# An encoder trunk on one core: the first projections of the sample before its norm, in an order written out by hand, and layer norm's last step on ScalarE

## The chip, the core and the metric

One core of one Trainium2 chip runs one launch of the whole network. The core has TensorE (PE, with its weight loads PEld), VectorE (DVE), ScalarE (ACT), GpSimd (POOL) and SyncE (SP, which here only issues transfers). The metric is the device time of the launch in microseconds. Everything is fp32 in memory; a product of two fp32 matrices is made on PE as three products of "high" and "low" parts (`hi` x `hi`, `lo` x `hi`, `hi` x `lo`), where `hi` is the number rounded to the fp32r format by an ACT copy, and `lo` what is left of it, by a subtraction on DVE or POOL.

## The reference, cut to what matters

There are two groups of tokens, a prompt of 1024 and a sample of 256, which pass the same layer. What the change touches is the layer's beginning:

```python
def rmsnorm(x, w):
    return x * lax.rsqrt(jnp.mean(x * x, -1, keepdims=True) + EPS) * w

h = rmsnorm(x, norm_mix_w)
proj = h @ w_in                     # columns: qkv, ab, dn_gate, sg_u, sg_v, gate_a, gate_b
...
u = gelu(sg_u)
v = layernorm(gelu(sg_v), ln_w, ln_b)
mixed = einsum('gts,bnsgc->bntgc', w_s, v) + b_s    # per chunk of 128 tokens
return u * mixed
```

The rest (gated DeltaNet over the qkv columns, branch gates, cross-attention into 256 memory tokens, a SwiGLU layer and a last norm) is the same in both kernels.

## The kernel before

**Tiles.** The model's 1024 features lie in `KT` = 8 slices `k` of 128 partitions, tokens along the free dimension. Tokens come in three blocks: `x0` and `x1` (512 tokens of the prompt each, blocks 0 and 1) and `xs` (the sample, block 2). `x_h[b]` holds the normed block as `hi` and `lo`. Chunks `c` are 128 tokens: 0 to 3 in block 0, 4 to 7 in block 1, 8 and 9 in block 2.

**The first stage.** It makes the sg_v columns and the 16 `ab` columns, with tokens as output rows (`sgv`, weights `w_sv` in two halves of 264 columns, tiles `svh`/`svl`), then the sg_u columns with features as output rows (`sgu(g, b)`, four weight tiles `w_u`). A chunk and half of `sgv` is a chain of 24 products of 264 columns into one PSUM bank (8 slices x 3), a tile and block of `sgu` one of 24 products of 512 or 256 columns. `gelu2` takes a bank out: a square on ACT, a step on DVE, a tanh on ACT, a step on DVE, which leaves `vg` (or `ug`). `ln` is the layer norm of `vg`: sums, four squares with accumulation on ACT, a root by Newton steps on DVE (`rsqrt`, ten tiny instructions), and at L458 the scaling of each chunk on DVE. `mix` multiplies a group of `vg` by the mixing weights `sw` on PE and ends in a store to `ybd`.

**A block's norm.** Squares on ACT are added up on DVE (`nacc`), PE sums them over partitions (a product with the column of ones, `bank<-cst,nacc`), DVE makes the root (`nst`), PE broadcasts it over the partitions (`bank<-cst,nst`), DVE scales each slice (`nt`, L285), ACT rounds it to `hi` and DVE or POOL subtracts for `lo` (`split`, L125 and L126; odd slices on DVE, even ones on POOL). `first_norm` does this for the sample at once; `other_norms` does block 0, then block 1, then the memory, beside the products.

**What sets the order.** PE's order is what the program writes. Main generators (`sgv`, `sgu`) yield after each slice, and side generators (norms, layer norms, mixes) are taken up when a clock that adds up nominal PE time has passed their due time (`K.clock`, `pump`; numbers such as `yield 3000` and `LAG0` are nanoseconds of it). `K.until` moves this clock on until a side generator has come to a point. The order on DVE, ACT, POOL and SP is made by a scheduler, from the program's order and estimated times. Each engine takes its instructions in order. The stage goes: `sgv` of the sample, `bias`, `sgu(0, 2)`, `sgu(1, 2)`; `sgv(0)`, `sgu(0, 0)`, `sgu(1, 0)`; `sgv(1)`, `decays`, `sgu(0, 1)`, `sgu(1, 1)`; then the tiles 2 and 3 for all blocks.

**Buffers.** PSUM banks for these products come from two pools of four (`pm` for `sgv` and `sgu`, `pq` for the rest). Raw weights have two buffers, `whi`/`wlo` two each, `nsq`/`nt` three, an x block one.

## Time and profile before

| | |
|---|---|
| time, median of 3 runs | 2236.44 us (2235.29 to 2237.58) |
| the profiled execution | 2239.41 us |
| its span | 2237.6 us |
| mean granted clock of PE | 0.996 |
| PE waits in the first 240 us, by releaser: DVE `nacc`, DMA `cst`, ACT `hi`, POOL `svl` | 8.6, 2.4, 2.3, 2.0 us |
| DMA over the span | 117 GB/s |

The profile is one execution: every instruction with its start and length, and for a wait the event that ended it. A group names the line in the code, the engine, output and inputs by their names in the program, and the shape. A line can be a helper's: L108 is every product, L125 and L126 every split. "Busy" of PE is a modelled figure in which neighbouring products overlap, so the step from one start to the next says more than a length. The granted clock says which share of TensorE's full clock the chip gave.

### The profile page before, as it was taken

To read this page: it belongs to the slowest core of one execution; us is meant where nothing else is said; L and a number is where in the kernel's file an instruction comes from. 1 tells how busy PE (TensorE), PEld (TensorE's weight loads), DVE (VectorE), ACT (ScalarE), POOL (GpSimd) and SP (SyncE) were. 2 spreads that over 40 slices of the span, in tenths; PEclk is the share of its full clock that TensorE was granted. 3 is DMA by queue.
4 is the path that set the end of the run, shared out by engine and by line. 5 is a ranking of instruction groups with operands and counts; after the bars stand their busy time and mean duration, and the time that the engine had idled before them with its cause. 6 is when DMAs were issued, how large, how long until landed. Compare 5 with 4: busy or idle time off the path is not lost.

```text
span 2237.6 us, 32329 instructions
## 1 busy us (share of the span) xinstructions
PE 2186.0 (98%) x12416; PEld 1909.1 (85%) x12416; DVE 1439.1 (64%) x2796; ACT 829.3 (37%) x1481; POOL 559.9 (25%) x358
## 2 busy tenths in 40 slices
PE   6999999999999999999999999999999999999998
PEld 5988888888888899788888888888888888888888
DVE  7767788897985874588844536743444344478575
ACT  5434143333423443124544433432223223243453
POOL 3010000000000000025331332466666666200031
PEclk9999999999999999999999999999999999999999
DMA  5222322214234454981431342222222222393531
GB/s 180 82 80 74 104 72 83 73 62 112 68 103 128 149 150 129 314 283 47 152 103 48 137 162 78 67 104 85 83 86 80 76 83 90 134 355 127 202 109 57
DMA packets 192821, 263.52 MB, mean 118 GB/s; under 512 B 72394, under 2 KB 102682, under 8 KB 192666
## 3 DMA queue, kind: packets, MB, share of 16 engines
q1 hardware_dynamic: 172826, 232.34, 31.7%
q10 hardware_dynamic: 19840, 29.11, 3.6%
q8 instruction: 97, 1.59, 0.3%
q14 instruction: 58, 0.48, 0.1%
HBM read 183.24 MB, written 78.16 MB: 117 GB/s over the span
## 4 chain that ended last, share of the span: by engine, by line
PE 77%; DVE 10%; issue 5%; DMA 4%; ACT 2%; POOL 1%; SPq 0%; ACTq 0%; POOLq 0%; DVEq 0%
PE bank L108 76%; DMA tbd<-stage 1%; PE bank L121 1%; DVE acc L615 1%; DVE xf L126 1%; DVE W L761 1%; DVE wlo L126 1%; DMA braw<-gq 1%; DVE x L1437 1%; DVE wlo L1228 1%; DMA t<-sgd 0%; DVE sw L919 0%; DVE W L764 0%; DVE U L861 0%; DVE lo L126 0%
## 5 line engine op out<-in xcount | busy, mean ns | idle before, releaser
L108 PE MATMUL bank<-hi,whi 128*128 128x512 f32 (+1 forms) x1976 | 701.8, 355 | 0.0
L108 PE MATMUL bank<-hi,wlo 128*128 128x512 f32 (+1 forms) x1976 | 687.0, 348 | 0.0
L108 PE MATMUL bank<-lo,whi 128*128 128x512 f32 (+1 forms) x1976 | 686.8, 348 | 0.0
L108 PEld LDWEIGHTS bank<-hi,wlo 128*128 128x128 f32 x1976 | 373.5, 189 | 48.8
L108 PEld LDWEIGHTS bank<-hi,whi 128*128 128x128 f32 x1976 | 374.4, 189 | 43.9 <-issue 0.2
L108 PEld LDWEIGHTS bank<-lo,whi 128*128 128x128 f32 x1976 | 374.5, 190 | 43.3 <-issue 0.2
L125 ACT ACTIVATE whi<-raw 128x1024 fp32r<-128x1024 f32 (+1 forms) x136 | 137.1, 1010 | 262.8 <-PE bank L108 221.4
L126 POOL TENSOR_TENSOR wlo<-raw,whi 128x1024 fp32r<-128x1024 f32 x65 | 157.5, 2426 | 302.8 <-ACT whi L125 302.8
L108 PE MATMUL bank<-bhl,whi 128*128 128x512 f32 x408 | 125.9, 390 | 0.0
L126 DVE TENSOR_TENSOR wlo<-raw,whi 128x1024 fp32r<-128x1024 f32 (+1 forms) x71 | 81.6, 1151 | 43.7 <-ACT whi L125 36.7
L126 POOL TENSOR_TENSOR wlo<-x,whi 128x1024 fp32r<-128x1024 f32 x40 | 97.5, 2436 | 46.8 <-ACT whi L125 46.7
L2009 DVE TENSOR_TENSOR x<-x,bank 128x512 f32<-128x512 f32 x21 | 14.4, 688 | 125.3 <-ACT x L1804 125.3
L108 PEld LDWEIGHTS bank<-bhl,whi 128*128 128x128 f32 x408 | 76.4, 188 | 16.3 <-ACT whi L125 0.3
L615 DVE SCALAR_TENSOR_TENSOR acc<-craw,sm,acc 128x510 f32<-128x510 f32 (+1 forms) x96 | 73.5, 766 | 20.5 <-ACT acc L613 19.1
L1817 DVE SCALAR_TENSOR_TENSOR t<-t,x 128x512 f32<-128x512 f32 x42 | 64.4, 1534 | 28.4 <-ACT t L1816 28.4
L108 PE MATMUL bank<-bhl,wlo 128*128 128x512 f32 x204 | 79.6, 390 | 0.5 <-DVE wlo L126 0.5
L761 DVE TENSOR_TENSOR W<-W,UT 128x2 f32<-128x2 f32 (+30 forms) x155 | 73.0, 471 | 11.0 <-DMA W<-in_eye 6.7
L250 DVE TENSOR_TENSOR nacc<-nacc,nsq 128x512 f32<-128x512 f32 (+1 forms) x68 | 57.9, 852 | 34.5 <-ACT nsq L249 33.4
L125 ACT ACTIVATE whi<-x 128x1024 fp32r<-128x1024 f32 (+1 forms) x48 | 49.0, 1025 | 79.9 <-PE bank L108 73.7
L1826 DVE SCALAR_TENSOR_TENSOR t<-bank,t 128x512 f32<-128x512 f32 (+1 forms) x44 | 24.5, 558 | 82.6 <-PE bank L108 82.6
L978 ACT ACTIVATE gs<-bank 128x512 f32<-128x512 f32 (+1 forms) x60 | 31.2, 520 | 124.9 <-PE bank L108 119.6
L881 POOL COPY UT<-U 64x512 f32<-64x512 f32 x20 | 13.9, 699 | 247.2 <-PE bank L108 245.6
(372 smaller groups left out, 4606.6 us busy)
## 6 DMA issues: line engine op xcount, KB each, us to landing
raw<-in_w_gu SPq DMA_DIRECT2D x44, 512.0 KB, 3.4
braw<-gq SPq DMA_DIRECT2D x14, 1024.0 KB, 6.5
raw<-in_w_g SPq DMA_DIRECT2D x20, 512.0 KB, 3.3
gq<-t SPq DMA_DIRECT2D x33, 256.0 KB, 2.0
gtd<-gs ACTq DMA_DIRECT2D x32, 256.0 KB, 2.0
w<-in_w_dn SPq DMA_DIRECT2D x8, 1024.0 KB, 12.3
raw<-in_w_qkv SPq DMA_DIRECT2D x12, 512.0 KB, 3.5
gq<-r SPq DMA_DIRECT2D x22, 256.0 KB, 2.1
```

What stands on the lines that cost most here:

```text
L108: self.nc.tensor.matmul(out, l, r, start=start, stop=stop, skip_group_check=more)
L121: self.nc.tensor.transpose(out, x, ident)
L125: self.last_hi = self.nc.scalar.activation(hi, src, AF.Copy).ins
L126: (eng or self.nc.vector).tensor_tensor(out=lo, in0=src, in1=f32(hi), op=ALU.subtract)
L250: (eng or V).tensor_tensor(out=self.acc, in0=self.acc, in1=sq, op=ALU.add)
L615: V.scalar_tensor_tensor(out=dst, in0=src, scalar=wj, in1=dst, op0=ALU.mult, op1=ALU.add)
L761: V.tensor_tensor(out=t3, in0=u3[:, i:, c:].rearrange("p j c -> p c j"), in1=XL[:, 32 * i + i : 32 * i + 32].unsqueeze(1).to_broadcast([P, ...
L978: S.activation(t, ps, AF.Tanh, scale=0.5)
L1228: eng.tensor_tensor(out=hl[1], in0=self.raw[*src, x], in1=f32(hl[0]), op=ALU.subtract)
L1437: V.scalar_tensor_tensor(out=d, in0=ps, scalar=0.5, in1=d, op0=ALU.mult, op1=ALU.add)
L1817: V.scalar_tensor_tensor(out=t, in0=t, scalar=1.0, in1=src, op0=ALU.add, op1=ALU.mult)
L1826: V.scalar_tensor_tensor(out=out, in0=u, scalar=sign, in1=t, op0=ALU.mult, op1=ALU.mult)
```

## The change

The sample's first projections are made from x * w, not from the normed h: rounding x times the norm's weight needs no root. The root of the token's mean square is multiplied in when the bank is read (`sample_evac`: a copy within PSUM scaled per partition; `gate_evac2`: a product with the broadcast root `rb2`). All of the stage from the first load up to the first half of `sgv(0)` stands in one stretch, `begin`, in which the orders on ACT, DVE, POOL and SP are also as the program writes them. In it the first half's raw weights are loaded from ACT's queue, the products of a group of banks run with slice `k` outermost (`sv_mm` over two chunks of the sample, over all four of block 0), and `sgu(0, 2)` and `sgu(1, 2)` come before block 0's products. The sample's own `hi` and `lo` of h are made later, by `other_norms`, ahead of x1's norm; block 0's norm is written out in the stretch. `LAG0` goes, and block 1 gets a lag `LAG1`. In `ln` the scaling becomes an ACT instruction, `Identity` with scale and bias, after one more tiny DVE step.

```diff
-            V.tensor_scalar(out=vg[:, c, :], in0=vg[:, c, :], scalar1=mu[:, c : c + 1], scalar2=rs[:, c : c + 1], op0=ALU.subtract, op1=ALU.mult)
+        V.scalar_tensor_tensor(out=mu[:, cs], in0=mu[:, cs], scalar=-1.0, in1=rs[:, cs], op0=ALU.mult, op1=ALU.mult)
+            S.activation(vg[:, c, :], vg[:, c, :], AF.Identity, scale=rs[:, c : c + 1], bias=mu[:, c : c + 1])
...
+    def sv_mm(pss, x, cols, w, k):
+        wh, wl = wk(w, k, 264)
+        for ps, cs in zip(pss, cols):
+            for n, (l, r) in enumerate(((x[0][:, k, cs], wh), (x[1][:, k, cs], wh), (x[0][:, k, cs], wl))):
+                mm(ps[:, :264], l, r, k == 0 and n == 0, k == KT - 1 and n == 2)
...
+    begin.enter_context(tc.manual_schedule(engines={S.engine, V.engine, G.engine, SY.engine}))
...
+    SY.dma_start(sm, a["small"])
+    for i, raw in enumerate(sv_raw0):
+        S.dma_start(raw, a["w_sv"][0][:, i * 1056 : (i + 1) * 1056])
...
+    for k in range(KT):
+        S.activation(xw[:, 0, k, :], xs[:, k, :], AF.Copy, scale=w_mix(k))
+        V.scalar_tensor_tensor(out=xw[:, 1, k, :], in0=xs[:, k, :], scalar=w_mix(k), in1=f32(xw[:, 0, k, :]), op0=ALU.mult, op1=ALU.subtract)
+    hl = sv_tiles()
+    for i in range(2):
+        sv_split(i, sv_raw0[i], hl)
...
+    ps2 = [[bank(pm) for _ in range(2)] for _ in range(2)]
+    for k in range(6):
+        sv_mm(ps2[0], x2w, cols2, sv[0], k)
...
+    u2(0)
+    pc0, nb0 = rstd_bank([sq0.acc], 512)
+    u2(1)
...
+    def sample_evac(half, i, ps):
+        c, nv = chunks(2)[i][0], 264 if half == 0 else 248
+        S.activation(ps[:, :264], ps[:, :264], AF.Copy, scale=y2[:, i : i + 1])
+        yield from gelu_of(ps[:, :nv], vg[:, c, half * 264 : half * 264 + nv], nv, (s0 if half == 0 else s1)[:, c : c + 1])
+        if half:
+            V.tensor_copy(ab[:, c, :], ps[:, 248:264])
...
+    go(0, 1, 0, 1)
+    rstd_col(pc0, nb0, y0)
+    go(2, 0, 1)
+    pb0 = rstd_rows(y0, 4)
+    steps = [(2,), (3,), (2,), (3, 4), (4, 3), (5, 4), (5,), (5,)]
...
+    for k in range(KT):
+        t = xp.tile([P, 512], F32, tag="nsq", name="nt", bufs=3)
+        V.scalar_tensor_tensor(out=t, in0=x0[:, k, :], scalar=w_mix(k), in1=pb0, op0=ALU.mult, op1=ALU.mult)
...
+        go(*steps[k])
...
+    V.tensor_scalar(out=h05, in0=sm[:, S_DNW : S_DNW + 9], scalar1=0.5, scalar2=None, op0=ALU.mult)
+    V.tensor_scalar(out=bias2, in0=bias2, scalar1=0.5, scalar2=None, op0=ALU.mult)
+    ps0 = [bank(pm) for _ in range(4)]
+    for k in range(KT):
+        sv_mm(ps0, x_h[0], [cs for _, cs in chunks(0)], sv[0], k)
+    begin.close()
...
+    def other_norms():
+        x1_ = x_load(a["xT"], 512, 512, "x1")
+        for k in range(KT):
+            t = xp.tile([P, 512], F32, tag="nsq", name="nt", bufs=3)[:, :NS]
+            V.scalar_tensor_tensor(out=t, in0=xs[:, k, :], scalar=w_mix(k), in1=rb2, op0=ALU.mult, op1=ALU.mult)
+            to_h(x_h, 2)(k, t)
+            yield 1500
+        done.add(2)
+        yield from norm(xp, lambda k: x1_[:, k, :], 512, S_MIX, to_h(x_h, 1), 900, lag=LAG1)
...
+    bias()
+    K.main(sgv(0, (1,)))
+    for b in (0, 1):
+        if b:
+            K.main(sgv(1))
+            K.side(decays())
+        K.main(sgu(0, b))
+        K.main(sgu(1, b))
...
-LAG0, LAGF, LAGF2, PACEF = 7500, (8000, 6000, 1500), (9000, 9000, 2800), 1000
+LAG1, LAGF, LAGF2, PACEF = 4000, (8000, 6000, 1500), (9000, 9000, 2800), 1000
```

How instructions move, at three places (a row is line, operation, output and inputs with buffer numbers, shape, and how often it repeats).

PE at the start, before: the mean square of the sample (`nacc`) and the broadcast of its root (`nst`), then one chunk's products with the normed `hi2` and `lo2`.

```order
L108 MATMUL bank_135<-cst_74,nacc_124 128x1 x4
L108 MATMUL bank_152<-cst_74,nst_140 128x128 x2
L108 MATMUL bank_212<-svh_104,hi2_101 128x264
L108 MATMUL bank_212<-svh_104,lo2_102 128x264
L108 MATMUL bank_212<-svl_103,hi2_101 128x264
```

PE at the start, now: `xw` is x * w, both of its parts under one name.

```order
L108 MATMUL bank_180<-svhi_162,xw_108 128x264 x2
L108 MATMUL bank_180<-svlo_163,xw_108 128x264
L108 MATMUL bank_181<-svhi_162,xw_108 128x264 x2
L108 MATMUL bank_181<-svlo_163,xw_108 128x264
L108 MATMUL bank_180<-svhi_162,xw_108 128x264 x2
L108 MATMUL bank_180<-svlo_163,xw_108 128x264
```

The two statistics groups moved behind products, and two banks take turns slice by slice.

DVE at the scaling of block 0 (`nt`, from `x0` and the broadcast in a bank), now: between the pieces stand the sample's gelu (`gt`, `vg`, `ug`) and the copies of `ab` out of the banks of its second half, `bank_182` and `bank_183`.

```order
L694 SCALAR_TENSOR_TENSOR nt_436<-x0_116,sm_75,bank_419 128x512
L700 TENSOR_TENSOR lo0_111<-nt_430,hi0_110 128x512
L663 SCALAR_TENSOR_TENSOR vg_100,sums_101<-gt_415,bank_182 128x248
L670 COPY ab_99<-bank_182 128x16
L694 SCALAR_TENSOR_TENSOR nt_443<-x0_116,sm_75,bank_419 128x512
L660 SCALAR_TENSOR_TENSOR gt_434<-gt_434,bank_183 128x248
L677 TENSOR_TENSOR ug_448<-bank_338,rb_119 128x256
L694 SCALAR_TENSOR_TENSOR nt_452<-x0_116,sm_75,bank_419 128x512
L700 TENSOR_TENSOR lo0_111<-nt_443,hi0_110 128x512
L660 SCALAR_TENSOR_TENSOR gt_450<-gt_450,ug_448 128x256
L663 SCALAR_TENSOR_TENSOR vg_100,sums_101<-gt_434,bank_183 128x248
L670 COPY ab_99<-bank_183 128x16
```

Before, only the sample's gate gelu and its layer norm stood between the pieces, and all of the sample's `sgv` banks were out by then.

PE at the mean square of x1, before: it stands (`nacc_556`) amid the products of block 0's second half, `bank_676`.

```order
L108 MATMUL bank_676<-svh_119,hi0_97 128x264
L108 MATMUL bank_676<-svh_119,lo0_98 128x264
L108 MATMUL bank_676<-svl_118,hi0_97 128x264
L108 MATMUL bank_692<-cst_74,nacc_556 128x1 x4
L108 MATMUL bank_676<-svh_119,hi0_97 128x264
L108 MATMUL bank_676<-svh_119,lo0_98 128x264
```

PE at the mean square of x1, now: it is `nacc_825`, the broadcast of its root is `nst_929`, and `hi1` and `lo1` are what this norm makes.

```order
L108 MATMUL bank_878<-hi0_110,whi_332 128x512
L108 MATMUL bank_878<-lo0_111,whi_332 128x512
L108 MATMUL bank_878<-hi0_110,wlo_333 128x512
L108 MATMUL bank_924<-cst_74,nacc_825 128x1 x4
L108 MATMUL bank_941<-sw_103,vg_100 128x128 x4
L108 MATMUL bank_950<-cst_74,nst_929 128x128 x4
L108 MATMUL bank_959<-sw_103,vg_100 128x128 x4
L108 MATMUL bank_1001<-svhi_162,hi1_112 128x264
L108 MATMUL bank_1001<-svhi_162,lo1_113 128x264
L108 MATMUL bank_1001<-svlo_163,hi1_112 128x264
```

It moved behind the last product of `sgu(1, 0)` (`bank_878`); between it and the first product with `hi1` stand only two mixes and the broadcast.

More of the change, by code (lines that the diff above doesn't have):

```diff
@@ L537, in bias @@
     def bias():
-        V.tensor_scalar(out=bias2, in0=bias2, scalar1=0.5, scalar2=None, op0=ALU.mult)
         pw = bank()
@@ L566, in sgu @@
         yield from proj(ps, ws[g], x_h, b)
[L567 removed]
+        if (g, b) in ((0, 1), (2, 2), (3, 2)):
             K.ahead()
@@ new lines, in rstd_rows, with __init__, square, add @@
+    def rstd_rows(y, nb):
+        pb = bank()
+        for c in range(nb):
+            mm(pb[:, c * P : (c + 1) * P], y[:, c : c + 1].to_broadcast([P, P]), ident)
+        return pb
+    class Squares:
+        def __init__(self):
+            self.acc = xp.tile([P, 512], F32, tag="nacc", name="nacc", bufs=2)
+            self.rest = []
+        def square(self, x):
+            t = self.acc if not self.rest else xp.tile([P, 512], F32, tag="nsq", name="nsq", bufs=3)
+            S.activation(t, x, AF.Square)
+            self.rest.append(t)
+        def add(self, k):
+            V.tensor_tensor(out=self.acc, in0=self.acc, in1=self.rest[k], op=ALU.add)
@@ new lines, in trunk_kernel @@
+    for k in range(4):
+        sv_mm(ps2[1], x2w, cols2, sv[1], k)
+    pb2 = rstd_rows(y2, 2)
+    for k in range(4, KT):
+        sv_mm(ps2[1], x2w, cols2, sv[1], k)
+    K.split_w(0)
+    for k in range(4, KT):
+        sq0.square(x0[:, k, :])
+        sq0.add(k - 2)
+    S.activation(rb2, pb2[:, :NS], AF.Copy)
+    K.lo_vector = True
+    sq0.add(6)
+    sq0.add(7)
+    K.split_w(1)
+    K.lo_vector = False
+    for g in range(2):
+        ws.append(K.take())
+    pu2 = [bank()[:, :NS] for _ in range(2)]
@@ L582, in trunk_kernel @@
         K.main(sgu(1, b))
+    K.until(norms, lambda: 2 in done)
     for g in (2, 3):
```

215 lines of the change are left out of this document (134 added, 81 removed).

## The prediction

> **What bounds the kernel now.** I read the page's engine line first, then the table of windows over the first 133 us (columns: stretch, length, busy us of PE, PEld, DVE, ACT and POOL with their instructions, granted PE clock, DMA share, GB/s), then the PE rows there in order of time, and last the groups by form.
>
> ```profile
> span 2237.6 us, 32329 instructions
> PE 2186.0 (98%) x12416; PEld 1909.1 (85%) x12416; DVE 1439.1 (64%) x2796; ACT 829.3 (37%) x1481; POOL 559.9 (25%) x358
> ...
> 0.00:16.00 16.00, 3.27 (x13) 2.92 (x13) 7.30 (x19) 6.65 (x9) 2.81 (x6) 1.00 0.86 301
> 16.00:44.40 28.40, 24.77 (x162) 22.99 (x163) 23.74 (x57) 17.07 (x35) 13.48 (x9) 0.94 0.37 129
> 44.40:57.00 12.60, 10.07 (x53) 8.58 (x52) 10.61 (x29) 6.89 (x15) 2.93 (x2) 0.73 0.46 158
> 57.00:115.60 58.60, 58.25 (x439) 55.91 (x439) 46.00 (x134) 27.75 (x61) 5.53 (x4) 1.00 0.24 88
> 115.60:133.00 17.40, 16.00 (x83) 13.03 (x82) 15.30 (x52) 8.28 (x18) 4.96 (x2) 1.00 0.17 58
> ```
>
> PE is busy for 98% of the span, so only what PE loses can be won, and most of it is lost in the first 57 us: in the three windows there PE is busy 38.1 of 57.0 us, partly at a lowered clock (0.94, 0.73). From 57 us on it is full. The change rewrites just this beginning. The order of the built programs differs on PE up to its instruction 620, the first product of `sgu(0, 1)`; from there PE's rows are the same in both. So I ask one thing: when does PE reach that instruction, which I call S? These rows of PE's timeline tell it for the kernel before (columns: start, duration, instruction, idle time before it and its releaser):
>
> ```profile
> 15.79 0.59 PE L108 MATMUL bank<-svh,hi 128*128 128x264 f32 x1 [1.79 <-ACT hi L125]
> ...
> 27.76 0.39 PE L108 MATMUL bank<-svl,hi 128*128 128x264 f32 x1 [2.03 <-POOL svl L126]
> ...
> 30.05 0.42 PE L108 MATMUL bank<-svl,hi 128*128 128x264 f32 x1
> 30.27 0.42 PE L108 MATMUL bank<-svh,hi 128*128 128x264 f32 x1
> ...
> 51.63 0.59 PE L108 MATMUL bank<-svh,lo 128*128 128x264 f32 x1
> ...
> 55.74 0.28 PE L108 MATMUL bank<-svh,lo 128*128 128x264 f32 x1
> 55.86 0.29 PE L108 MATMUL bank<-svl,hi 128*128 128x264 f32 x1
> ...
> 65.24 0.95 PE L108 MATMUL bank<-cst,nacc 128*128 128x1 f32 x8
> ...
> 87.09 0.39 PE L108 MATMUL bank<-hi,whi 128*128 128x512 f32 x1
> 87.32 0.39 PE L108 MATMUL bank<-lo,whi 128*128 128x512 f32 x1
> ...
> 115.62 0.40 PE L108 MATMUL bank<-hi,whi 128*128 128x512 f32 x1
> ```
>
> The reader sees four things. The first projection starts at 15.79, after the mean square and its root. S is at 115.62. A 264-column product follows the one before it by 0.12 us (55.74, 55.86), and by 0.22 us where the clock is low (30.05, 30.27); a 512-column one by 0.227. And after a stall the low clock stays on: dense work resumes at 51.63 and has the short step only from 55.74, 4.1 us later; half of that, some 2 us of work, is lost.
>
> **The start.** The first projection now takes x*w and needs no root: it needs the small table, all four pieces of the sample's x and the first half of the weights, whose two loads move to ACT's queue.
>
> ```profile
> GB/s 0 0 81 291 328 232 327 249 268 293 349 352 369 394 401 406 412 401 388 391 347 414 382 363 227 108 176 281 205 46 0 0 0 0 0 0 0 0 131 360
> ...
> raw<-in_w_sv SPq DMA_DIRECT2D x4, 528.0 KB, 6.4
> ...
> xs<-in_xT SPq DMA_DIRECT2D x4, 256.0 KB, 3.7
> ...
> sm<-in_small SPq DMA_DIRECT2D x1, 54.5 KB, 4.2
> ```
>
> That is 4 x 256 + 2 x 528 + 54.5 KB, 2.19 MB. The GB/s row has 0.75 us slots; its running sum reaches 2.08 MB at 9.0 us and 2.19 at 9.3. At the later rate of some 400 it would be 7.0. Then come two last ACT pieces of x*w, the weight's high half on ACT and its low half on DVE; the groups of ACT by form (busy, mean ns of one) and a row of DVE's timeline give their prices:
>
> ```profile
> L125 ACT ACTIVATE hi<-nt 128x512 fp32r<-128x512 f32 x16 | 9.9, 631 | 6.9 <-DVE nt L285 6.7
> ...
> L125 ACT ACTIVATE svh<-raw 128x1056 fp32r<-128x1056 f32 x4 | 4.3, 1075 | 3.1 <-DMA raw<-in_w_sv 3.1
> ...
> L125 ACT ACTIVATE hi<-nt 128x256 fp32r<-128x256 f32 x8 | 3.2, 413 | 4.5 <-DVE nt L285 4.5
> ```
>
> ```profile
> 28.18 1.25 DVE L126 TENSOR_TENSOR svl<-raw,svh 128x1056 fp32r<-128x1056 f32 x1
> ```
>
> With x in at 9.0, a little ahead of the weights on the other queue, the first product stands at 10.7 (two pieces 0.7, the high half 1.08) and dense work begins a low half later: 12.0; by 400 GB/s it is 10.1. I take 11.8, since the slots up to 9 us are the nearest rows and some of the split lies under the last load. In the page "DMA: Bandwidth & Descriptors", section "Issuing engines are not separate DMA queues", the Trainium skill says that loads issued by several engines run on the same 16 DMA engines and interleave, and only the issuing time is saved; by that the move to ACT's queue brings nothing to 11.8, and no run here yet shows two such queues at the start.
>
> Up to the end of the broadcast of block 0's root PE then has 142 products (17.1), two mean groups and two broadcasts (2.6, an estimate from 0.95 us for the group of four at 65.24, half for the sample's), and about 22 products at the low clock (22 x 0.1 = 2.2): 33.7. Squares, splits and the new readout by the root (four ACT copies and two DVE products) lie beside these products. The closest is the second gate weight's low half: on DVE it stands behind the sample's root, a weight split (1.25) and six sums, and ends near 28, two us ahead of its product; past that, each microsecond it is late is one of PE's.
>
> **Block 0.** Here PE starves. DVE's order after the broadcast puts scaled pieces of x0, low halves and the sample's gelu in one line. Its groups by form (busy, mean ns of one):
>
> ```profile
> L285 DVE SCALAR_TENSOR_TENSOR nt<-x,sm,bank 128x512 f32<-128x512 f32 x16 | 11.4, 740 | 1.7 <-issue 1.3 <-PE bank L108 0.4
> ...
> L427 DVE SCALAR_TENSOR_TENSOR gt<-gt,bank 128x248 f32<-128x248 f32 x10 | 4.1, 407 | 3.1 <-ACT gt L426 3.1
> ...
> L429 DVE SCALAR_TENSOR_TENSOR vg<-gt,bank 128x248 f32<-128x248 f32 x10 | 4.1, 410 | 1.1 <-ACT gt L428 1.0
> ...
> L126 DVE TENSOR_TENSOR lo<-nt,hi 128x512 fp32r<-128x512 f32 x8 | 5.5, 684 | 0.0
> ...
> L533 DVE COPY ab<-bank 128x16 f32<-128x16 f32 x10 | 1.7, 168 | 0.0
> ...
> L553 DVE SCALAR_TENSOR_TENSOR mx<-bank,h,bias 128x512 f32<-128x512 f32 x3 | 2.2, 749 | 0.1
> ```
>
> With the contraction outermost, all four banks of block 0 are written in the first step, and the fourth bank is the one that holds the sample's last half: it comes free at the copy of `ab` out of `bank_183`, fifteenth in that line. Before it: 5 pieces (0.74), 2 low halves (0.68), 6 gelu steps of 0.41 and 2 copies (0.17), 7.9 us by the means, less some 0.07 for each overlap, 7.0. So from 34.0 PE makes 9 products and stands until 41.3; by then four of eight steps are ready and DVE stays ahead. The other 87 products take 10.5, the low clock 2.2: 54.0. The kernel before is there at 65.24 less 15 products, 63.4, and has by then done 1.4 us of bias and mixes that now come later. So the beginning brings 8.0 us.
>
> Behind the last low half DVE still has `h05`, `bias2` and the sample's own h pieces, some 6 us (an estimate, at half the prices of the 512 forms), before it comes to block 0's gelu. PE's remaining steps cover them, from 47 to 54; uncovered they would cost what is over.
>
> Next the second half waits for a bank: gelu of the first chunk takes four steps of about 0.4, 1.5 us with the bias product under it. A gap of 1.1 us stays; the rows before show that 2.03 us of it (27.76) was followed by the low clock (30.05), price 1.6. I take nothing, keeping 1.6 for the range. On this gap the Trainium skill ("TensorE: Matmul & The Clock Gate", section "Part 1: The HAM clock gate (the "warmup" mystery)") says that the clock falls after about 3.4 us of idleness; the trace disagrees at 27.76, where 2.03 us were enough. By the rule the gap is free, by the row it may cost 1.6.
>
> The rest of block 0: 96 products 11.6, 48 of 512 columns 10.9, two mixes 0.9. PE then stands at 78.9, at the end of `sgu(1, 0)`.
>
> **x1, the new wait.** In the kernel before, x1's norm ran under block 0's products:
>
> ```profile
> 66.82 0.17 DVE L228 TENSOR_TENSOR bank<-bank,nst 128x4 f32<-128x4 f32 x1
> ...
> 70.60 1.41 DVE L285 SCALAR_TENSOR_TENSOR nt<-x,sm,bank 128x512 f32<-128x512 f32 x2 [1.30 <-issue]
> ...
> 80.43 0.69 DVE L126 TENSOR_TENSOR lo<-nt,hi 128x512 fp32r<-128x512 f32 x1
> ```
>
> The first of these is one tiny step of the root (they follow each other by 0.2), the second the first scaled pieces, the third the last low half. From the mean product (65.24, above) to 81.12 it took 15.9 us and nobody waited. In the change its generator starts later and first makes the sample's eight h pieces, so PE's order has the mean product only *behind* `sgu(1, 0)`, directly before `sgv(1)`: the cover is gone. The chain now: mean product 0.95; root, eleven steps of 0.2, with a mix, two gelu steps and a gate product (0.75 + 3 x 0.68) put between them on DVE, 5.0; broadcast 1.2; and eight pieces with their halves, 10.5 as at 70.60 to 81.12, since the same number of foreign steps lies between: 17.8. PE can do 6.3 in that time (mean 0.8, broadcast 0.9, two mixes 0.9 each, 24 products 2.9) and ends its first chunk at 18.1: 11.8 lost, then 2.2 at the low clock. Bounds: 12.5 for the chain with nothing between (0.95 + 2.2 + 1.2 + 8 x 0.67 + 4 x 0.6 + 0.4), and 19.5 as block 0's own norm took in the kernel before:
>
> ```profile
> 32.06 0.95 PE L108 MATMUL bank<-cst,nacc 128*128 128x1 f32 x8
> ...
> 50.88 0.69 DVE L126 TENSOR_TENSOR lo<-nt,hi 128x512 fp32r<-128x512 f32 x1
> ```
>
> I take 17.8, close to both measured ones. Behind it 168 products (20.2), the memory's mean and broadcast (1.7) and the low clock (2.2): S at 78.9 + 18.1 + 24.1 = 121.1, against 115.6.
>
> **After S.** Layer norm's end moves from DVE to ACT. In block 1 it stood on PE's way once:
>
> ```profile
> 130.75 1.40 PE L108 MATMUL bank<-sw,vg 128*128 128x128 f32 x6 [1.32 <-DVE vg L458]
> ...
> 127.66 3.95 DVE L458 TENSOR_SCALAR vg<-vg,sums 128x512 f32<-128x512 f32 x4
> ...
> 122.40 2.35 DVE L228 TENSOR_TENSOR sums<-sums 128x4 f32<-128x4 f32 x1
> ```
>
> The four scalings took 3.95 us on DVE, and a tiny step 2.35 beside a POOL split. On ACT four take about 2.5 (4 x 0.63, the shape of `hi`). But the next gate weight's split now stands on ACT between the four squares that the variance needs, and that split waits for PE to finish `sgu(0, 1)`, 5.5 us after S; the variance comes some 2 us later than before. I set both against each other: nothing (from 1.3 won to 1.0 lost).
>
> **Sum.** 121.1 - 115.6 = +5.5. On the profiled execution (2239.4 us, of which 2237.6 are span) that makes 2244.9; the runs' median is 3.0 lower, so I forecast 2242. In parts: the beginning brings 8.0; the bank's gap takes 1.1 and x1 11.8 + 2.2; the kernel before lost some 1.5 of its own between 63.4 and S, which falls away.
>
> **Rivals.** (1) *x1's chain at its bare length.* If DVE gets through the foreign steps while it waits, the chain is 12.5, PE loses 6.5 instead of 11.8, and the clock holds: +5.5 - 5.3 - 2.2 = -2.0, 2234. For it: ACT and POOL have room there. Against: DVE's order is fixed, and in both norms before DVE was full. Below some 14 us from mean product to last half the change isn't slower. Chance 0.17. (2) *Both starvations as long as block 0's in the kernel before*: 19.5 for x1 (+1.7), 1 more for block 0, and the gap of 1.1 trips the clock (1.6): +9.8, 2246. For it: the tiny steps that stood 1 to 2 us beside POOL. Chance 0.15. (3) *The start is sooner*, by two queues at 400 GB/s: 1.7 less, +3.8, 2240. Against: the same 16 engines carry both. Chance 0.08. (4) *The clock never falls* in the three stalls: 6.6 less, -1.1, 2235; against it stand 30.05 and 51.63. Chance 0.05. That the order isn't what the words say is excluded by the order itself.
>
> **Chances.** The forecast has 0.55; its own range is +2 to +10. A measurement of this kernel tells 0.2%, 4.5 us, from no change. Forecast: 0.50 slower, 0.05 same. Rival 2: 0.15 slower. Rival 1: 0.08 same, 0.07 faster, 0.02 slower. Rival 3: 0.07 same, 0.01 slower. Rival 4: 0.02 same, 0.03 faster. Together 0.68, 0.22, 0.10. The range runs from 2233 (rival 1 less the 1 us that the runs spread) to 2251 (rival 2 with the high start, the microsecond after S, the low clock half as long again at both stalls, and the spread).
>
> **What would show it.** First projection at 10 to 11 us, a stall of PE from about 34 to 41 us released by DVE, a second idle stretch at about 80 to 97 us with releasers `nst`, `hi` and `lo` and the clock down, S at about 121. Wrong would be: x1's mean product early and no stall at 80 us, or S before 115, or different idle time after S.

## The result, and the profile after

| | before | after |
|---|---|---|
| median of the runs | 2235.87 us (4 runs) | 2255.53 us (4 runs, 2254.66 to 2260.51) |
| ratio, 95% interval | | 1.0091 (1.0074 to 1.0109): slower by 0.9% |
| profiled execution, its span | 2239.41, 2237.6 us | 2255.55, 2253.7 us |

The forecast was 2242 us, in a range of 2233 to 2251: the sign was right, the size was not. The page of the changed kernel:

```profile
span 2253.7 us, 32347 instructions
PE 2194.6 (97%) x12416; PEld 1915.9 (85%) x12416; DVE 1440.5 (64%) x2802; ACT 841.1 (37%) x1504; POOL 546.9 (24%) x355
```

PE's work is the same (12416 products), so the 16.1 us between the spans are waits and a lowered clock. The table of windows of the changed kernel shows where (columns as before: stretch, length, busy us of PE, PEld, DVE, ACT, POOL, granted clock, DMA share, GB/s):

```profile
38.00:57.00 19.00, 15.70 (x97) 15.22 (x98) 18.76 (x44) 12.48 (x29) 8.43 (x8) 0.73 0.33 112
57.00:82.00 25.00, 24.44 (x155) 21.73 (x154) 16.72 (x70) 16.68 (x39) 0.00 (x0) 1.00 0.03 11
82.00:102.30 20.30, 13.11 (x55) 10.62 (x54) 14.58 (x29) 7.42 (x12) 5.92 (x4) 0.62 0.09 31
...
125.40:146.40 21.00, 17.06 (x80) 13.72 (x78) 16.90 (x55) 11.09 (x22) 4.74 (x2) 0.88 0.41 149
146.40:153.30 6.90, 6.90 (x25) 5.74 (x25) 2.42 (x6) 0.80 (x2) 0.00 (x0) 0.62 0.10 39
```

Three stretches are bad. In 38 to 57 us PE starves at block 0, as forecast. In 82 to 102.3 it is busy 13.1 of 20.3 us at a clock of 0.62: x1's norm, also forecast. And in 125.4 to 153.3, behind S (now 125.38), it loses time again, with the clock at 0.88 and 0.62; the forecast had nothing there. In the kernel before, the same products behind S stand in these windows at full clock:

```profile
115.60:132.60 17.00, 15.60 (x81) 12.68 (x79) 15.20 (x51) 8.01 (x18) 4.96 (x2) 1.00 0.16 51
132.60:137.10 4.50, 4.50 (x24) 3.85 (x25) 2.85 (x6) 1.07 (x3) 0.00 (x0) 1.00 0.30 114
```

So the loss is +9.8 us at S (125.38 against 115.62), and +16.2 where the products of `sgu(0, 2)`'s two mixes begin (153.25 against 137.09); from there both of these executions need 2100.5 us to the end. The rows of PE, first of the start and of block 0:

```profile
7.06 1.28 ACT L605 ACT_TABLE_LOAD   x1 [7.06 <-DMA xs<-in_xT]
8.35 3.30 ACT L605 ACTIVATE xw<-xs,sm 128x256 fp32r<-128x256 f32 x8
...
12.68 0.81 PE L108 MATMUL bank<-svhi,xw 128*128 128x264 f32 x2 [12.68 <-ACT svhi L125]
13.97 0.59 PE L108 MATMUL bank<-svlo,xw 128*128 128x264 f32 x1 [0.48 <-DVE svlo L126]
...
38.07 0.39 PE L108 MATMUL bank<-svhi,hi 128*128 128x264 f32 x1 [1.50 <-ACT hi L699]
39.44 0.59 PE L108 MATMUL bank<-svhi,lo 128*128 128x264 f32 x1 [0.98 <-POOL lo L700]
43.82 0.56 PE L108 MATMUL bank<-svhi,hi 128*128 128x264 f32 x1 [2.25 <-ACT gt L661]
...
56.92 1.02 PE L108 MATMUL bank<-sw,cst 128*128 128x512 f32 x2
```

The first line is ACT's load of its function table, 1.28 us. It stands in ACT's line behind the first wait for x, so it lies on the path; in the kernel before it lay under the loads. The first product comes at 12.68, dense work at 13.97. The fourth bank keeps PE idle until 43.82 (the row names ACT's `gt`, but what reads that bank last is DVE's copy of `ab`, 43.51 to 43.67), and block 0's first half ends at 56.92. Next, x1's rows and S:

```profile
82.03 0.95 PE L108 MATMUL bank<-cst,nacc 128*128 128x1 f32 x8
87.77 2.05 PE L108 MATMUL bank<-cst,nst 128*128 128x128 f32 x8 [3.79 <-DVE nst L229]
...
96.33 0.59 PE L108 MATMUL bank<-svhi,hi 128*128 128x264 f32 x1 [1.06 <-ACT hi L125]
97.58 0.59 PE L108 MATMUL bank<-svhi,lo 128*128 128x264 f32 x1 [0.67 <-DVE lo L126]
...
125.38 0.40 PE L108 MATMUL bank<-hi,whi 128*128 128x512 f32 x1
```

The mean product stands at 82.03, as the order said, though VectorE had finished its input long before: the last sum of x1's squares ran at 66.26 (0.69 us). The chain then runs with little of PE's work beside it, to 102.1. And behind S, first DVE's rows, then PE's:

```profile
129.44 0.74 DVE L285 SCALAR_TENSOR_TENSOR nt<-mem,sm,bank 128x512 f32<-128x512 f32 x1
130.97 0.65 DVE L285 SCALAR_TENSOR_TENSOR nt<-mem,sm,bank 128x512 f32<-128x512 f32 x1
132.35 2.40 DVE L421 TENSOR_TENSOR wk<-wk 128x80 f32<-128x80 f32 x1
...
138.50 2.32 DVE L228 TENSOR_TENSOR sums<-sums 128x4 f32<-128x4 f32 x1
...
140.73 0.44 DVE L431 SCALAR_TENSOR_TENSOR gm<-wk,rows 128x32 f32<-128x32 f32 x4
```

```profile
141.05 0.78 PE L108 MATMUL bank<-cst,gm 128*40 128x128 f32 x4 [2.82 <-DVE gm L431]
142.93 2.91 PE L108 MATMUL bank<-sw,vg 128*128 128x128 f32 x8 [1.11 <-ACT vg L392]
146.41 0.43 PE L121 MATMUL bank<-cst,gr 40*128 40x40 f32 x2
...
153.25 1.05 PE L108 MATMUL bank<-sw,vg 128*128 128x128 f32 x8
```

The scaled pieces of the *memory's* norm (`nt<-mem`, eight, five of them behind S) stand in DVE's line in front of the steps of `decays()` (`wk`) and of layer norm (`sums`). In the kernel before all eight were done by 113.75, ahead of S. Two tiny steps stand 2.3 to 2.4 us each beside a weight split on POOL; in the kernel before it was one (122.40, 2.35). So `gm` comes at 140.73, 15.4 us behind S instead of 10.4, PE waits 2.82 for it and 1.11 for `vg`, and the clock falls.

### The profile page after: what moved, and what is told of

Same layout as the page of the kernel before. It is cut to its first block, busy times and chain, and to the rows that moved or that the text cites. A ratio compares the mean times of both kernels' runs of the same rounds, so it can differ in the third digit from the quotient of the medians.

```text
span 2253.7 us, 32347 instructions
## 1 busy us (share of the span) xinstructions
PE 2194.6 (97%) x12416; PEld 1915.9 (85%) x12416; DVE 1440.5 (64%) x2802; ACT 841.1 (37%) x1504; POOL 546.9 (24%) x355
## 4 chain that ended last, share of the span: by engine, by line
PE 78%; DVE 9%; issue 6%; DMA 3%; ACT 2%; POOL 1%; POOLq 0%; SPq 0%; ACTq 0%; DVEq 0%
PE bank L108 77%; DMA tbd<-stage 2%; PE bank L121 1%; DVE acc L778 1%; DVE wlo L126 1%; DVE xf L126 1%; DVE x L1600 1%; DVE U L1024 1%; DVE wlo L1391 1%; DVE sw L1082 0%; DMA t<-sgd 0%; DVE nt L285 0%; DVE aT L893 0%; DVE zt L1016 0%; DVE lo L126 0%
## 5 line engine op out<-in xcount | busy, mean ns | idle before, releaser
L108 PEld LDWEIGHTS bank<-lo,whi 128*128 128x128 f32 x1960 | 372.7, 190 | 43.4
L2172 DVE TENSOR_TENSOR x<-x,bank 128x512 f32<-128x512 f32 x21 | 14.4, 688 | 125.4 <-ACT x L1967 125.4
L778 DVE SCALAR_TENSOR_TENSOR acc<-craw,sm,acc 128x510 f32<-128x510 f32 (+1 forms) x96 | 73.6, 766 | 20.3 <-ACT acc L776 18.8
L108 PE MATMUL bank<-bhl,ahl 128*128 128x512 f32 x312 | 75.0, 395 | 0.0
## 6 DMA issues: line engine op xcount, KB each, us to landing
w<-in_w_dn SPq DMA_DIRECT2D x8, 1024.0 KB, 13.1
```

Of the source, the lines that this page charges most:

```text
L108: self.nc.tensor.matmul(out, l, r, start=start, stop=stop, skip_group_check=more)
L778: V.scalar_tensor_tensor(out=dst, in0=src, scalar=wj, in1=dst, op0=ALU.mult, op1=ALU.add)
```

## Experiments

Each kernel was run beside the kernel before on the same chip. That kernel's median lay between 2235.9 and 2238.4 from one set of runs to the next, so ratios compare better than medians. S is read from each run's trace. A trace is one execution, and executions part again behind S although PE's order there is the same: the trace of bank is 3.7 us ahead of the changed kernel's at S and 0.4 at the end (spans 2253.3 and 2253.7), that of table 0.7 and 3.3 (2250.4). At 299.5 to 302.1 us, for example, products of 512 columns follow each other by 0.43 us in bank's trace and by 0.23 in the changed kernel's. So S tells where a loss lies, and the ratio what it is worth.

| kernel | median us | ratio to before, 95% interval | S us | S to `gr` us |
|---|---|---|---|---|
| before | | | 115.62 | 16.98 |
| after | 2255.53 | 1.0091 (1.0074 to 1.0109) | 125.38 | 21.03 |
| x1_early | 2248.01 | 1.0039 (1.0022 to 1.0057) | 119.08 | 20.59 |
| mem_late | 2247.69 | 1.0040 (1.0026 to 1.0054) | 124.16 | 16.76 |
| ln_dve | 2253.25 | 1.0068 (1.0053 to 1.0083) | 125.78 | 19.85 |
| k_inner | 2260.32 | 1.0095 (1.0080 to 1.0110) | 127.90 | 21.06 |
| x1_mem | 2244.64 | 1.0029 (1.0017 to 1.0042) | 115.58 | 16.76 |
| x1_mem_mix | 2237.84 | 0.9999 (0.9988 to 1.0010) | 114.27 | 16.76 |
| table | 2252.82 | 1.0072 (1.0051 to 1.0093) | 124.66 | 21.03 |
| bank | 2251.69 | 1.0063 (1.0044 to 1.0082) | 121.67 | 21.03 |
| before_ln_act | 2240.37 | 1.0013 (1.0002 to 1.0024) | 118.62 | 16.73 |
| before_mem_late | 2236.91 | 0.9996 (0.9987 to 1.0005) | 110.71 | 16.98 |
| all | 2239.79 | 1.0008 (1.0000 to 1.0017) | 115.76 | 16.76 |
| all_ln_dve | 2245.04 | 1.0029 (1.0018 to 1.0041) | 117.88 | 17.01 |
| all_mean | 2239.89 | 1.0013 (1.0003 to 1.0024) | 113.39 | 16.76 |
| all_mean_pace | 2235.27 | 0.9997 (0.9987 to 1.0006) | 111.61 | 16.76 |

(`gr`: the two transposes behind `gm`, the last mark that stands at nearly the same place in all. Where the memory's norm is late, its mean product and broadcast, 1.8 us, come behind S and `gr` instead of ahead of S.)

**x1_early**: x1's mean product sooner in PE's order.

```diff
-            yield 1500
+            yield 300
         done.add(2)
-        yield from norm(xp, lambda k: x1_[:, k, :], 512, S_MIX, to_h(x_h, 1), 900, lag=LAG1)
+        yield from norm(xp, lambda k: x1_[:, k, :], 512, S_MIX, to_h(x_h, 1), 900, 500, lag=LAG1)
-LAG1, LAGF, LAGF2, PACEF = 4000, (8000, 6000, 1500), (9000, 9000, 2800), 1000
+LAG1, LAGF, LAGF2, PACEF = 300, (8000, 6000, 1500), (9000, 9000, 2800), 1000
```

> The pauses in the side job that makes the sample's h pieces and x1's norm are cut (1500 to 300, 700 to 500, and the lag before the mean product 4000 to 300), so that x1's mean product stands some 78 places sooner in TensorE's order, in front of sgu(0, 0) instead of behind sgu(1, 0); the work is the same. Theory (the loss is where TensorE's order puts x1's mean product; its sum of squares was complete at 66.9 us and lay idle until 82.0): mean product at 67 to 69 us, the eight pieces at 73 to 86, the idle stretch of TensorE between 87 and 101 us and its low clock gone but for 1 to 2 us, S (first product of sgu(0, 1), 125.4 in the changed kernel) at 111 to 115; time 2239 to 2245, 11 to 16 less than the changed kernel. Rival (x1's chain is limited by VectorE and GpSimd, wherever it stands): the pieces still come as slowly and push gelu behind them, S at 119 or later, time 2250 or more.

Half of it held. PE's rows:

```profile
68.39 0.95 PE L108 MATMUL bank<-cst,nacc 128*128 128x1 f32 x8
...
86.50 0.40 PE L108 MATMUL bank<-svhi,lo 128*128 128x264 f32 x1 [0.23 <-DVE lo L126]
90.63 2.91 PE L108 MATMUL bank<-sw,vg 128*128 128x128 f32 x8 [3.62 <-ACT vg L392]
...
136.19 2.91 PE L108 MATMUL bank<-sw,vg 128*128 128x128 f32 x8 [3.49 <-ACT vg L392]
```

x1's wait is gone but for 0.23 us: its chain fits under `sgu(0, 0)` and `sgu(1, 0)`. In its place stands a wait of 3.62 us for `vg`: block 0's layer norm now shares DVE and ACT with x1's pieces, its four activations on ACT start only at 89.77, and PE's order has the mix that needs them right there. x1's pieces take from 74.4 to 89.7 instead of 73 to 86. S comes at 119.1, the rival's mark, and 3.49 us for `vg` stay behind it; the time lies between the two ranges. The ratio fell by half a per cent all the same.

**mem_late, ln_dve, before_mem_late**: what is lost behind S?

```diff
         mem = x_load(a["memT"], 0, 512, "mem")
-        yield 6000
+        yield 26000
```

> The changed kernel with the memory's norm put off (one pause of 6000 made 26000), so that its eight scaled pieces no longer stand in VectorE's line in front of decays() and of layer norm's variance for block 1. Theory A (after S TensorE loses 6.4 us more than before because those eight pieces, 0.74 us each, push gm and the variance back): TensorE's idle time for gm at 141.05 us and for vg at 142.93 goes, the stretch from S to the product of sgu(0, 2)'s two mixes (27.9 us, 21.5 in the kernel before) falls to 22 to 24, time 2249 to 2252. Rival B (the stall comes from layer norm's end on ScalarE): gm comes sooner but vg does not, the stretch stays at 26 to 28, time within 2 us of 2255.5.

> The changed kernel with layer norm's end back on VectorE (four tensor_scalar instead of the tiny product and four Identity activations), all else as it is. Theory A (the memory's pieces are what delays gm and vg): the four scalings take some 3.95 us on VectorE instead of 2.93 on ScalarE, so TensorE's wait for vg is the same or 1 to 2 us longer; time 2255 to 2258. Rival B (layer norm's end on ScalarE is the cause): the stretch from S to the two mixes falls from 27.9 to 22 to 24, time 2249 to 2251.

In mem_late, `gm` and the transposes are on time again:

```profile
136.93 0.63 PE L108 MATMUL bank<-cst,gm 128*40 128x128 f32 x4
...
139.39 0.49 PE L108 MATMUL bank<-sw,vg 128*128 128x128 f32 x2 [0.22 <-ACT vg L392]
140.92 0.31 PE L121 MATMUL bank<-cst,gr 40*128 40x40 f32 x2 [0.68 <-DVE gr L439]
```

S to `gr` fell from 21.03 to 16.76 us, S to the two mixes from 27.9 to 22.1, and the clock stays at 1.00 from 110 to 160: theory A. The time fell by somewhat more than A said. In ln_dve both waits stayed (2.85 for `gm`, 0.80 for `vg`): the engine of layer norm's end is not the main cause. But the median fell by 2.3 us, between the two theories (the ratio by 0.23%, with intervals that overlap), and S to the two mixes is 24.9: the larger part of the 3.0 us gained there lies behind the transposes of `gr`, where the clock came back sooner.

The control, with the same edit (34000) in the kernel before:

> The kernel before with the memory's norm put off in the same way as in mem_late, to the same place in TensorE's order behind decays(). Theory (the memory's pieces cost only where they fall between S and gm; in the kernel before they lay at 109 to 114 us, ahead of S): at most 1.5 us won, the idle time of 1.32 us for vg at 130.75; time 2235.5 to 2238. Rival (putting them off is worth the same in either kernel): 2230 to 2232, 6 us or more won.

2236.91, a ratio of 0.9996: putting off the memory's norm is worth nothing where it is on time. So mem_late's gain is the repair of a delay that the change made. (S in this trace is 4.9 us sooner for other reasons: 1.8 are the memory's two groups of products, which now come later, and 2.5 a stall at 27 us behind which the clock held, see the last section.)

**before_ln_act**: the change's edit of `ln` alone, in the kernel before.

> The kernel before with layer norm's end alone moved to ScalarE (the tiny product and the four Identity activations of the change). My forecast's step: nothing, between 1.3 won and 1.0 lost. Theory after ln_dve (there the way back gave 2.3): 0 to 2.5 us lost, time 2237.5 to 2240. Rival (the move costs only where the norm comes late, behind the memory's pieces): within 1 of the kernel before.

0.13% slower (0.02 to 0.24), the theory's side. The trace (the slowest of its ten executions) shows where: behind S nothing is lost (S to the two mixes 21.2 us, 21.5 before), but PE's products of block 0's mix now follow ACT's activations one by one, with 0.42 and three times about 0.22 us idle at 90.66 to 92.77, where the kernel before had no wait. The clock falls behind these short gaps (the column before the last two), where it was 1.00 before, and S comes 3.0 us later.

```profile
90.00:95.00 5.00, 3.93 (x19) 3.15 (x19) 3.31 (x6) 3.30 (x6) 0.00 (x0) 0.82 0.01 3
95.00:100.00 5.00, 5.00 (x37) 5.00 (x37) 1.59 (x6) 1.05 (x3) 0.00 (x0) 0.84 0.14 52
```

**k_inner, bank, table**: the parts of the start. As a measure: in the traces of six kernels whose order on PE is the same up to there (the changed one, x1_early, mem_late, ln_dve, x1_mem, x1_mem_mix), block 0's first half ends between 55.9 and 57.3 us.

```diff
-    for k in range(KT):
-        sv_mm(ps0, x_h[0], [cs for _, cs in chunks(0)], sv[0], k)
+    for ps, (_, cs) in zip(ps0, chunks(0)):
+        for k in range(KT):
+            sv_mm([ps], x_h[0], [cs], sv[0], k)
```

> The changed kernel with block 0's first half chunk by chunk again (the contraction innermost), all else as it is. My theory of the start: TensorE then takes three products per piece of x0 while the pieces come (about 1.4 us each, the last low half at 49 us), and has 72 products left then (8.7 us and 2 at the low clock): block 0's first half ends at 59 to 61 us instead of 57, in return the wait of 2.25 us for the fourth bank goes; time 2257 to 2260. Rival (x1's chain alone sets S, since its sum of squares is complete 15 us before its mean product): S and the time move with the end of block 0 all the same, as TensorE's order has them in one line; so a time unchanged within 1 us would say that the contraction's order is worth nothing.

Block 0's half ended at 59.85 instead of 56.92, as expected. S came 2.5 us later; the median rose by 4.8, the ratio by 0.04% only, which can't be told from nothing. The contraction outermost is worth some 2.5 us in the trace; in the time it isn't shown.

```diff
-    steps = [(2,), (3,), (2,), (3, 4), (4, 3), (5, 4), (5,), (5,)]
+    steps = [(2, 3), (2, 3), (3,), (4,), (4,), (5, 4), (5,), (5,)]
```

> The changed kernel with the sample's gelu steps among x0's pieces put in another order, so that the copy of ab out of the sample's last bank stands behind three of x0's pieces instead of five; the rest of the sample's steps comes later, the work is the same. Theory (block 0's fourth bank is what TensorE waited for at 43.8 us): the wait of 2.25 us goes or shrinks below 0.7, and block 0's first half ends at 54 to 55.5 us instead of 56.9; time 2252.5 to 2254. Rival (VectorE's line is full, so x0's pieces come later by the steps that are put ahead): TensorE waits for pieces instead, and the half ends within 0.7 us of 56.9.

```profile
38.21 0.39 PE L108 MATMUL bank<-svhi,hi 128*128 128x264 f32 x1 [1.50 <-ACT hi L699]
39.57 0.59 PE L108 MATMUL bank<-svhi,lo 128*128 128x264 f32 x1 [0.97 <-POOL lo L700]
52.73 1.02 PE L108 MATMUL bank<-sw,cst 128*128 128x512 f32 x2
```

No wait is left between 39.57 and 52.73, and the half ends 4.2 us sooner, more than the wait of 2.25: the clock falls less too (0.72 in 40 to 45 us and 1.00 in 45 to 50, where the changed kernel has 0.50 and 0.58). S gains 3.7.

```diff
+    V.memset(h05[:, 0:1], 1.0)
+    S.activation(h05[:, 0:1], h05[:, 0:1], AF.Square)
```

> The changed kernel with one activation of a single column at its very start, of a constant that VectorE writes, ahead of the first that waits for a load; so the table of functions (7.06 to 8.34 us in the changed kernel, 1.28 us, 0.73 us in the kernel before) is loaded while the data come. Theory: first product at 11.3 to 11.5 us instead of 12.7, and everything up to S 1.0 to 1.3 sooner; time 2253.5 to 2254.8. Rival (the loads set the start): ScalarE then waits for the pieces of x, and the first product moves by less than 0.5.

```profile
1.65 1.28 ACT L583 ACT_TABLE_LOAD   x1 [1.65 <-PEq L2498]
...
7.15 3.30 ACT L608 ACTIVATE xw<-xs,sm 128x256 fp32r<-128x256 f32 x8 [4.00 <-DMA xs<-in_xT]
```

The table is in at 2.93, ACT works from 7.15, the first product stands at 11.48 (1.2 sooner). But S gains only 0.7, less than kernels of the same order differ by: block 0's chain follows the root of its own squares, and that came 0.5 sooner (mean product at 31.24 instead of 31.76).

**x1_mem, x1_mem_mix**: the edits together, and then

```diff
-MIX = 6500
+MIX = 12000
```

> x1's mean product early (as in x1_early) and the memory's norm late (as in mem_late) together. In x1_early S came at 119.1 us, after which TensorE still stood 3.5 us for vg; in mem_late the wait after S went. Theory (two separate losses, S by x1's place and the stretch after S by the memory's pieces): S at 118 to 120, the stretch from S to the product of sgu(0, 2)'s two mixes 21 to 23 us (26.0 in x1_early), time 2240 to 2244; TensorE's wait of 3.6 us for vg at 90.6 us stays, since block 0's layer norm still shares VectorE with x1's pieces. Rival (one loss that two edits each took in part): 2245 or more.

> x1_mem with the pause between a layer norm and the mixes that read it lengthened (6500 to 12000), so that block 0's first mix stands behind some 45 of sgv(1)'s products in TensorE's order; the work is the same. Theory: in x1_early TensorE stood at 90.6 us for vg (3.62 us idle, then some 2.5 us at the low clock) only because the mix was put in front of work that was ready; that goes, S at 112 to 115, time 2234 to 2239, no more than the kernel before. Rival (block 0's layer norm is late in any case and the wait moves): a wait for vg or for a bank of 2 us or more at 92 to 100 us, time 2240 or more.

x1_mem took both gains in part (0.29%; S at 115.6, lower than expected, and the wait of 3.63 us for `vg` at 89.3). With the mixes later that wait was gone as well and the time is that of the kernel before: 0.9999. Of the rival's wait, 2.75 us for `hi` and `lo` of x1 remain at 86 to 90. So with three side jobs placed otherwise in PE's order (x1's norm, the memory's norm, the mixes) the whole 0.9% is gone. (Later mixes and an earlier x1 were not tried in the kernel before.)

**all, all_ln_dve**: x1_mem_mix with table and bank.

> The changed kernel with four edits together: x1's mean product early, the memory's norm late, mixes later (x1_mem_mix: 2237.8), the table's early load (table: 2.7 sooner than the changed kernel) and the other order of the sample's gelu steps (bank: 3.8 sooner). Theory (they are separate losses): first product at 11.4 us, no wait for block 0's fourth bank, time 2230 to 2234, less than the kernel before by 3 to 7. Rival (what the start wins is lost at x1, whose sum of squares then isn't complete when TensorE comes to its mean product, and whose pieces come no sooner): TensorE waits 2 us or more for nacc, hi or lo between 64 and 92 us, time 2235 to 2238.

> The kernel called all with layer norm's end back on VectorE. Theory: with the mixes put off nothing waits for layer norm's end, so its engine makes no difference: within 1.5 of all. Rival (ScalarE's four activations lie in the way of x1's high halves and of gelu): 2 us or more sooner than all.

Neither range held. The start is 5.8 us sooner at block 0's end (51.13), and then:

```profile
66.41 1.87 PE L108 MATMUL bank<-cst,nacc 128*128 128x1 f32 x8 [3.90 <-DVE nacc L250]
```

The rival's mark: PE reaches the mean product before x1's sum of squares is there, waits 3.90 us and runs on at the low clock (0.50 in 65 to 70). S is 115.8, later than without the better start. In the changed kernel bank and table had ratios lower by 0.28 and 0.19% (their intervals still overlap that of the changed kernel); there x1's mean product only waits for PE to arrive. Here PE arrives first, and what the start won is lost. With layer norm's end on DVE it got worse, against both theories: the wait is 4.78 in a trace whose execution (2239.52 us) is one of the fastest. That DVE's scalings, which lie in the line of those sums, do it is argued, not shown.

**all_mean, all_mean_pace**: the mean product 24 places later (pauses 100, 700 and a lag of 300); then also the pause between x1's pieces 500 instead of 900.

> The kernel called all with x1's mean product 24 places later in TensorE's order (in front of sgu(0, 0)'s third product instead of inside sgv(0)), so that TensorE has work until the sum of squares is complete at some 66 us. Theory (all lost the start's gain in the wait of 3.90 us for nacc at 66.41 and the low clock after it, both for the place of one product): the mean product at 66 to 69 us without a wait over 0.5, clock 1.00 from 65 to 75, S at 111 to 114 (115.7 in all), time 2234 to 2238. Rival (x1's chain is bound by when x1's data and squares are ready, since x1 is loaded into x0's buffer; the stall only moves to x1's pieces in front of sgv(1)): TensorE waits 3 us or more for hi or lo at 77 to 92 us, S at 115 or later, time 2239 to 2242.

> The kernel called all_mean with the pause between x1's pieces cut (900 to 500), so that fewer foreign steps lie between them on VectorE. Theory: what TensorE still waits for x1's pieces falls by 1 to 2 us; time 0 to 2 under all_mean. Rival (GpSimd's low halves, 1.3 us each, set the pace): within 1 of all_mean.

```profile
66.77 1.05 PE L108 MATMUL bank<-cst,nacc 128*128 128x1 f32 x8 [0.33 <-DVE nacc L250]
...
80.58 0.39 PE L108 MATMUL bank<-svhi,lo 128*128 128x264 f32 x1 [0.41 <-POOL lo L126]
82.59 0.58 PE L108 MATMUL bank<-svhi,lo 128*128 128x264 f32 x1 [1.38 <-DVE lo L126]
84.81 0.59 PE L108 MATMUL bank<-svhi,hi 128*128 128x264 f32 x1 [1.42 <-ACT hi L125]
86.17 0.59 PE L108 MATMUL bank<-svhi,lo 128*128 128x264 f32 x1 [0.77 <-POOL lo L126]
```

Both expectations are half right: the wait for `nacc` fell to 0.33 and S to 113.4, as the theory had it, but four waits for x1's halves, 3.98 us together, stand at 80 to 87, as the rival had it, and the median did not move (2239.89). all_mean_pace has the same four waits (4.2 us), yet it was 4.6 us faster. In its trace the clock is back at 1.00 from 90 us, in all_mean at 95, and S is 1.8 us sooner; the rest of the 4.6 is not explained. At 0.9997 (0.9987 to 1.0006) it has the lowest ratio of the changed kernels, and isn't told apart from x1_mem_mix or from the kernel before. None beat that kernel.

## Why the prediction was wrong

Step by step, forecast and measured, in the changed kernel's trace:

| step | forecast | measured |
|---|---|---|
| first product, dense work | 10.7, 11.8 | 12.68, 13.97 |
| end of the broadcast of block 0's root | 33.7 | 36.6 |
| fourth bank free | 41.3 | 43.8 |
| block 0's first half done | 54.0 | 56.9 |
| end of `sgu(1, 0)` | 78.9 | 82.0 |
| S | 121.1 (+5.5) | 125.4 (+9.8) |
| loss behind S | 0 (1.3 won to 1.0 lost) | 6.4 |

**The step that failed is "After S ... nothing".** The forecast weighed layer norm's four activations against a weight split on ACT, 1 to 2 us each way, and so looked only at what the edit of `ln` touches. What decided was a job that the change had not edited: with x1's norm late, the memory's norm starts later too, and its eight pieces of 0.74 us came into DVE's line in front of `gm` and the variance. The stretch from S to the two mixes took 6.4 us more than before instead of the same. The forecast even counted the memory's mean and broadcast ahead of S, but not who would stand behind its pieces. mem_late, which gives 5.8 of the 6.4 us back, and its control show it. "Different idle time after S", which it named as a sign that it is wrong, is what appeared. The two prices that it weighed did come to nothing behind S (before_ln_act, 21.2 us for 21.5); what the activations cost, 0.13%, arose ahead of S, at block 0's mix, where the forecast had not looked for it.

**The start was mis-sized by 2.2 us** (dense 13.97 for 11.8). The terms that failed are ACT's, not the loads'. The windows of 3 to 9 us, after and before, show

```profile
3.00:9.00 6.00, 0.00 (x0) 0.00 (x0) 0.11 (x1) 1.93 (x3) 0.00 (x0) 1.00 1.06 376
3.00:9.00 6.00, 0.45 (x2) 0.45 (x3) 2.16 (x4) 2.52 (x4) 0.00 (x0) 1.00 0.93 300
```

376 GB/s where the kernel before had 300, with two queues at work; whether the second queue did it wasn't tried. But the sample's x came in no sooner than forecast: its four loads, issued at 1.2 to 3.0 us, landed after 5.9 us (median), the first at 7.0 and the last at about 8.9, where the forecast had 9.0. With that agrees the rule of the Trainium skill in "DMA: Bandwidth & Descriptors", section "Issuing engines are not separate DMA queues", by which only the issuing time is saved. Behind the loads the forecast put two last pieces of x*w (0.7) and the high half. What stood there was ACT's table (1.28 from 7.06 on, a term that it had at nothing), then all eight pieces (3.30) and the high half (1.08), one after another.

**Block 0 was right**: from the broadcast to the half's end 20.3 us forecast, 20.4 measured, with the fourth bank as the wait. The gap behind it was 0.56 us instead of 1.1, and the clock held there. The forecast's own sum is loose here by 0.3 us (34.0 + 7.0 is 41.0, not 41.3).

**x1 was right in mechanism; its size came out near in part by luck.** From the end of `sgu(1, 0)` to S 42.2 us were forecast, 43.4 measured, but two errors cancel in that. The chain was longer: 20.1 us from the mean product to the last half instead of 17.8 (the broadcast 2.2 for 1.2, since it runs at the low clock, the pieces 12.2 for 10.5), so that the first chunk ended after 20.8 instead of 18.1. What follows was shorter, 22.6 for 24.1. The clock was at 0.62 over 20 us. The Trainium skill's figure of about 3.4 us of idleness before the clock falls ("TensorE: Matmul & The Clock Gate", section "Part 1: The HAM clock gate (the "warmup" mystery)") agrees with x1's wait, where 3.79 us of it stood ahead, but not with block 0's: there 1.50 and 0.98 us had been idle and the clock was 0.50 in 40 to 45 us.

**From profile to median.** The forecast took 3.0 us off its sum. The changed kernel's profiled execution lies at its median instead, while that of the kernel before lay 3.5 us above its own; so 3 us of the error are in this step. The account of the error, 13.5 us: 6.4 behind S, 4.3 ahead of S (2.2 start, 1.2 x1, the rest in pieces under 1), 3 here; these add up to 13.7, the difference being rounding.

Of the rivals, the second came nearest (starvations longer and the clock tripped, 2246). Its +9.8 at S is even the measured one, but by luck: of its parts only the longer chain of x1 came (19.5, measured 20.1), block 0 wasn't longer, the gap behind it didn't trip the clock, and the late start made up the sum. Behind S it had nothing either.

## What to carry to other kernels

When a change moves one job in an order that a planner's clock spreads out, list every side job that hangs on it, to its last instruction, and ask in whose line these will now stand; the loss behind S came from a job whose code was untouched. A mean product that stands in PE's order 15 us behind its ready input is a loss like a late input (x1_early: a ratio lower by 0.5% with it sooner). And a faster beginning is worth only as much as the next block's side job can follow: x1's sum of squares was there at 66 to 67 us whether block 0 ended at 51 (all) or at 57 (the changed kernel), though x1's last load had landed at about 54 and 56; its squares and sums stand among gelu and layer norm steps in ACT's and DVE's lines. An engine's one-time setup, as ACT's table here, should stand ahead of its first wait (1.2 us at the first product).

## What the hardware showed that was not expected

**One stall, two outcomes of the clock.** Up to the memory's mean product, at 99 us in the kernel before, that kernel and before_mem_late have the same order on PE. The windows from 25 to 35 us of the first, then of the second with its stall:

```profile
25.00:30.00 5.00, 2.97 (x19) 2.76 (x18) 4.90 (x5) 2.34 (x6) 2.71 (x1) 0.84 0.20 74
30.00:35.00 5.00, 5.00 (x38) 5.00 (x37) 3.32 (x18) 2.62 (x6) 1.03 (x1) 0.82 0.44 141
```

```profile
27.12 0.39 PE L108 MATMUL bank<-svl,hi 128*128 128x264 f32 x1 [1.64 <-POOL svl L126]
```

```profile
25.00:30.00 5.00, 3.36 (x26) 2.95 (x25) 5.00 (x6) 1.93 (x6) 2.07 (x1) 1.00 0.33 107
30.00:35.00 5.00, 5.00 (x39) 4.52 (x38) 3.40 (x20) 3.63 (x7) 2.94 (x2) 1.00 0.34 108
```

A wait of 2.03 us at 27.76 (shown above) was followed by a clock of 0.82 to 0.84, one of 1.64 us at 27.12 by none. before_ln_act had 1.77 there and 0.83. x1's mean product then stood at 65.24, 62.78 and 64.95. So one stall decides over 2 us. Its length does not settle the outcome: behind S both kernels wait the same 1.32 us for `vg`, and the clock stays at 1.00 in the kernel before (130.75, both shown above), but falls to 0.76 in before_mem_late:

```profile
125.85 1.40 PE L108 MATMUL bank<-sw,vg 128*128 128x128 f32 x6 [1.32 <-DVE vg L458]
...
125.00:130.00 5.00, 4.07 (x19) 3.37 (x20) 4.63 (x9) 0.83 (x2) 0.51 (x1) 0.76 0.36 116
```

What decides isn't shown here; a forecast that prices such a stall needs both outcomes.

**Tiny DVE steps beside a POOL split** took 2.3 to 2.4 us instead of 0.15 to 0.24, twice in one line here, and four `wk` steps took 3.15 us in x1_early where three had taken 0.80. Each of the long steps began at most 0.1 us after the split and ended with it (132.35 to 134.75 us, the split 132.25 to 134.65).
